# Low parts of two weight operands per pair: from a VectorE subtraction to a ScalarE negation and an adding DMA

## The chip, the cores and the metric

The kernel runs on one NeuronCore of a Trainium2 chip. The metric is the device time of one launch in microseconds, as the median of several runs. The engines are named as the profile names them: PE (TensorE, matrix products), DVE (VectorE), ACT (ScalarE), POOL (GpSimd) and SP (SyncE, which here only issues DMAs). Each engine takes its own instructions strictly in their order and waits on semaphores of the others; an instruction that waits holds up everything behind it on its engine.

## The reference

One layer of a hybrid encoder over 512 tokens of width 1024, in float32: a token-mixing part (a bidirectional Mamba-2 scan, dilated window attention, gates, a projection), a LayerNorm, and a channel part. The change lies in the channel part alone:

```python
h = layer_norm(alpha * h + mix, ln1_g, ln1_b)
f = jnp.square(jax.nn.relu(h @ w_up)) @ w_down      # w_up: 1024 x 4096, w_down: 4096 x 1024
h = layer_norm(alpha * h + f, ln2_g, ln2_b)
```

## The kernel before

**Split operands.** PE multiplies in a reduced float32 form (fp32r). To keep the accuracy, every operand `w` is split into a high part `h`, which is `w` rounded to fp32r, and a low part `l = w - h`; a product is then three PE products, high by high, high by low and low by high. The helper `wsplit` (L1298 to L1300) makes such a pair: ACT copies (casts) the source into `h`, DVE subtracts `f32(h)` from the source into `l`.

**The pairs.** The first blocks of `w_up` are multiplied plainly. The rest go in 14 pairs of 128-column blocks, `PAIRS`, numbered n = 0 to 13. A pair is computed as a 2 x 2 block product with seven multiplications in place of eight. Its two blocks are loaded raw (`pair_load`, L1281) into `pr{n}_0` and `pr{n}_1`, tiles of 128 x 1024 in a pool of three buffers. `pair_prep(n, e)` makes the weight operands out of them in four steps:

- e = 0: `pa{n}`, high and low part of the whole of `pr{n}_0`.
- e = 1: `pb{n}`, two sums. Here `pr{n}_0` and `pr{n}_1` are changed in place by four additions on DVE (L1315, L1317, L1319, L1321), of which L1315 is the first that needs `pr{n}_1`; the high parts are ACT casts (L1316, L1320), the low parts DVE subtractions (L1318, L1322).
- e = 2: `pc{n}`, high and low part of `pr{n}_1` as it is by then (128 x 1024); after it, `pair_load(n + 1, 1)` reuses the buffer of `pr{n}_1`.
- e = 3: `pd{n}`, high and low part of the second half of `pr{n}_0` (128 x 512); after it, `pair_load(n + 2, 0)` reuses that buffer.

Steps 2 and 3 are the third and fourth operand, and both call `wsplit`.

**Their use.** `up_seg(n, 0..3)` issues the PE work of a pair: 12 matmuls of 256 columns per multiplication, eight with the high part of the weights and then four with the low part. Segment 0 uses `pa`, segment 1 `pb`, segment 2 `pc`, segment 3 `pd`. The PSUM tiles are `ps_x{n}` (two banks in turn), `ps_y` and `ps_z` (one bank each). All of a pair's x products accumulate in one tile, and its intermediate sums are read out of it on the way: ACT reads it after segment 1 (L1381) and DVE after segment 2 (L1390), and PE may go on adding to it only after that. ReLU and square are ACT operations in place (L1354, L1355, L1373, L1396, L1397).

**The down products.** Between the segments of the pairs stand the products with `w_down`, also seven to a 2 x 2 block scheme, for three chunks of 1024 hidden columns (`product`, L169 to L171: 12 matmuls of 512 columns for each half of the weights, j = 0 and j = 1). Their activations are split into `ah` and `al` (L1450 on ACT, L1451 on DVE), their weights into `ch` and `cl`, once for each j (L1456 on ACT, L1457 on DVE). The weight sums between the products are made by adding DMAs: `add_halves` (L1425) lets POOL issue a DMA that adds one raw quarter of `w_down` to another in SBUF (`wq_B` tiles, 512 KB each).

**What sets the order.** The loop at the end of the page interleaves pairs and products. PE's order is the order of the program text there. The orders of ACT, DVE, POOL and SP in this stage come from a scheduler, which at build time lists the instructions by its own estimate of when each is due; on the chip each engine then follows its list, whatever the real times are. POOL issues nothing in this stage but the adding DMAs.

Of the kernel before, what the change touches and what calls it, by code (L numbers as in the profile page):

```python
# [11 lines left out]
F32R = mybir.dt.float32r  # L12
AF = mybir.ActivationFunctionType
ALU = mybir.AluOpType
# [27 lines left out]
def f32(ap):  # L42
    return ap.bitcast(F32)
# [3 lines left out]
def hybrid_layer_kernel(ctx: ExitStack, tc: tile.TileContext, t: dict, out: bass.AP):  # L47
    nc = tc.nc
    act, dve, pool, pe, dma = nc.scalar, nc.vector, nc.gpsimd, nc.tensor, nc.sync
# [1227 lines left out]
    def pair_load(n, j):  # L1277
        if n < len(PAIRS):
            ch, b = PAIRS[n]
            raw_w[n, j] = wp.tile([P, 1024], F32, name=f"pr{n}_{j}", tag="wraw", bufs=3)  # L1280
            dma.dma_start(raw_w[n, j], t["w_up"][ch * 8 + b + j])  # L1281
# [4 lines left out]
    def slot(name):  # L1286
        if name in LENT:
            both = qp.tile([P, 2, 1024], F32R, name=name, tag=f"wq{LENT[name]}", bufs=1)
            return both[:, 0, :], both[:, 1, :]
        if name in ("pb0", "pc1"):  # L1290
            return [qp.tile([P, 1024], F32R, name=f"{name}{x}", tag=f"c{x}", bufs=2) for x in "hl"]
        s_ = slot_n[0] % 3
        slot_n[0] += 1
        if s_ < 2:
            return [wp.tile([P, 1024], F32R, name=f"{name}{x}", tag=f"w{x}", bufs=2) for x in "hl"]
        return [fp.tile([P, 1024], F32R, name=f"{name}{x}", tag=f"x{x}", bufs=1) for x in "hl"]

    def wsplit(h, l, src):  # L1298
        act.copy(h, src)
        dve.tensor_sub(l, src, f32(h))  # L1300

    K0, K1 = slice(0, 512), slice(512, 1024)

    def pair_prep(n, e):

        if n >= len(PAIRS):
            return
        r0, r1 = raw_w[n, 0], raw_w.get((n, 1))
        if e == 0:
            h, l = slot(f"pa{n}")  # L1310
            wsplit(h, l, r0)
            op_w[n, "B11"], op_w[n, "B21"] = (h, l, K0), (h, l, K1)
        elif e == 1:
            h, l = slot(f"pb{n}")
            dve.tensor_add(r0[:, K0], r0[:, K0], r1[:, K0])  # L1315
            act.copy(h[:, K0], r0[:, K0])  # L1316
            dve.tensor_add(r1[:, K0], r1[:, K0], r1[:, K1])  # L1317
            dve.tensor_sub(l[:, K0], r0[:, K0], f32(h[:, K0]))  # L1318
            dve.tensor_add(r0[:, K0], r0[:, K0], r1[:, K1])  # L1319
            act.copy(h[:, K1], r0[:, K0])  # L1320
            dve.tensor_add(r0[:, K1], r0[:, K1], r0[:, K0])  # L1321
            dve.tensor_sub(l[:, K1], r0[:, K0], f32(h[:, K1]))  # L1322
            op_w[n, "T1"], op_w[n, "T2"] = (h, l, K0), (h, l, K1)
        elif e == 2:
            h, l = slot(f"pc{n}")
            wsplit(h, l, r1)
            op_w[n, "T3"], op_w[n, "B22"] = (h, l, K0), (h, l, K1)
            pair_load(n + 1, 1)
        else:
            h, l = slot(f"pd{n}")  # L1330
            wsplit(h[:, K0], l[:, K0], r0[:, K1])
            op_w[n, "T4"] = (h, l, K0)
            pair_load(n + 2, 0)

# [174 lines left out]
    with tc.issue_after(ln_end[-1].ins):  # L1509
        pair_prep(0, 0)  # L1510
    hf_ctx.close()
    qp = wq_ctx.enter_context(tc.tile_pool(name="qp", bufs=1, side="right", reuse_waits="tile"))
    with tc.issue_after(ln_end[-1].ins):
        pair_prep(0, 1)
# [3 lines left out]
    with tc.manual_schedule(engines={mybir.EngineType.PE}):  # L1518
        up_seg(0, 0)
        pair_prep(0, 2)  # L1520
        up_seg(0, 1)
        pair_prep(0, 3)
        pair_prep(1, 0)
        up_seg(0, 2)
        load_quarter(0, "B12")
        up_seg(1, 0)
        pair_prep(1, 1)
        load_quarter(0, "B22")
        up_seg(0, 3)
        pair_prep(1, 2)  # L1530
        up_seg(1, 1)
        pair_prep(1, 3)
        ops = split(0, SEQ[0])
        pair_prep(2, 0)
        up_seg(1, 2)
        up_seg(2, 0)
        pair_prep(2, 1)
        up_seg(1, 3)
        load_quarter(0, "B21")
        sums(0, SEQ[0])  # L1540
# [161 lines left out]
```

## Time and profile before

| | |
|---|---|
| median of 3 runs | 984.01 us (983.98 to 986.72) |
| the profiled execution | 984.42 us, span of its instructions 982.7 us |
| PE busy | 972.9 us (99% of the span) |
| DVE busy | 806.5 us (82%) |
| ACT busy | 607.2 us (62%) |
| POOL busy | 76.2 us (8%) |
| granted PE clock | 0.999 of full speed |

All times inside the execution count from the span's start, in microseconds. In a row of the timeline the first number is the start, the second the duration; then come engine, line, operation, the tile written, `<-`, the tiles read, shapes, and in brackets the idle time of the engine before it with what ended it. Buffer numbers are often left out by the profile (`pr` for `pr4_1`), so a row is placed by its time. A row of SPq is the issue of a DMA; the landing time is given separately. The pairs run from about 670 to 932 us.

### The profile page before, as it was taken

The page shows a single profiled execution, that of the slowest core. Times are in us where ns is not written, and L with a number is a line of the kernel's source. Part 1 is how long each engine was busy: PE and PEld are TensorE (multiplying, and loading weights), DVE is VectorE, ACT ScalarE, POOL GpSimd, SP SyncE. Part 2 cuts the span into 40 slices and gives each one's busy share as a digit, 9 for nine tenths or more (in the row PEclk, how much of TensorE's full clock was granted, in tenths as well). Part 3 has the DMA queues.
Part 4 walks back from the last instruction along what each step waited for, and adds up shares of the span by engine and source line. Part 5 has one row for each costly group of instructions (what it writes and reads, how often), then busy time and mean ns, then how long its engine had stood idle before and what let it go on. Part 6 is the DMA issues. An engine that isn't in the chain of part 4 may idle for free.

```text
span 982.7 us, 14783 instructions
## 1 busy us (share of the span) xinstructions
PE 972.9 (99%) x5447; PEld 835.1 (85%) x5447; DVE 806.5 (82%) x1235; ACT 607.2 (62%) x1149; POOL 76.2 (8%) x79
## 2 busy tenths in 40 slices
PE   9999999999999999999999999999999999999997
PEld 6988888888888888788778888899989998989986
DVE  7986998798998899997798258498898898898757
ACT  6664796469856995694775344147666666656620
POOL 0100100120011101202000000000200110110000
PEclk9999999999999999999999999999999999999999
DMA  9666476335652485474773248313953854671322
GB/s 355 152 146 171 127 199 199 97 116 153 214 151 90 149 243 147 123 234 140 252 237 111 79 149 313 127 44 125 242 148 131 213 129 171 176 169 44 110 83 86
DMA packets 57992, 155.94 MB, mean 159 GB/s; under 512 B 7488, under 2 KB 10432, under 8 KB 57664
## 3 DMA queue, kind: packets, MB, share of 16 engines
q1 hardware_dynamic: 53072, 139.04, 43.9%
q0 software_dynamic: 4560, 15.44, 8.6%
q8 instruction: 43, 0.70, 0.3%
q10 hardware_dynamic: 288, 0.52, 0.1%
q14 instruction: 29, 0.24, 0.1%
HBM read 128.25 MB, written 12.44 MB: 143 GB/s over the span
## 4 chain that ended last, share of the span: by engine, by line
PE 86%; DVE 8%; ACT 3%; DMA 2%; issue 1%; DVEq 0%; SPq 0%; ACTq 0%
PE ps_pa L159 9%; PE ps_z L159 8%; PE ps_x L159 8%; PE ps_x L1341 8%; PE ps_z L1341 4%; PE ps_k L159 3%; PE ps_g L159 3%; PE ps_q L159 3%; PE ps_pX L169 2%; PE ps_pX L170 2%; PE ps_pX L171 2%; PE ps_y L1341 2%; PE ps_vX L351 2%; PE ps_u L159 2%; PE ps_pZ L169 2%; PE ps_pZ L170 2%
## 5 line engine op out<-in xcount | busy, mean ns | idle before, releaser
L110 DVE TENSOR_TENSOR wl<-wraw,wh 128x1024 fp32r<-128x1024 f32 x103 | 129.7, 1265 | 57.4 <-ACT wh L109 42.2
L109 ACT CAST wh<-wraw 128x1024 fp32r<-128x1024 f32 x103 | 107.2, 1045 | 73.9 <-PE ps_o L171 13.2
L1457 DVE TENSOR_TENSOR cl<-wq_B,ch 128x1024 fp32r<-128x1024 f32 x42 | 51.2, 1220 | 14.8 <-ACT ch L1456 14.3
L1456 ACT CAST ch<-wq_B 128x1024 fp32r<-128x1024 f32 x42 | 44.1, 1050 | 24.0 <-PE ps_pX L171 16.6
L159 PE MATMUL ps_pa<-yh,wh 128*128 128x512 f32 x128 | 51.7, 404 | 0.0
L1425 POOL DMA_DIRECT2D wq_B<-wq_B x24 | 20.6, 856 | 391.2 <-DMA wq_B<-in_w_dn_dram 225.4
L159 PE MATMUL ps_g<-xh,wh 128*128 128x512 f32 x128 | 50.6, 396 | 0.0
L159 PE MATMUL ps_z<-xh,wh 128*128 128x512 f32 x128 | 50.4, 393 | 0.0
L159 PE MATMUL ps_g<-xl,wh 128*128 128x512 f32 x128 | 49.9, 390 | 0.0
L159 PE MATMUL ps_z<-xl,wh 128*128 128x512 f32 x128 | 49.9, 389 | 0.0
L159 PE MATMUL ps_pa<-yl,wh 128*128 128x512 f32 x128 | 48.4, 393 | 0.0
L724 ACT ACTIVATE U<-bc,acr 128x128 f32<-128x128 f32 x128 | 42.3, 391 | 8.9 <-DMA bc<-dr_acr 7.7
L159 PE MATMUL ps_x<-xh,wh 128*128 128x512 f32 x120 | 47.2, 394 | 0.0
L159 PE MATMUL ps_x<-xl,wh 128*128 128x512 f32 x120 | 46.7, 389 | 0.0
L522 DVE SCALAR_TENSOR_TENSOR acc<-ps_x,vec,acc 128x510 f32<-128x510 f32 (+1 forms) x60 | 44.5, 742 | 0.7 <-ACT acc L520 0.3
L726 DVE SCALAR_TENSOR_TENSOR U<-bc,acr,U 128x128 f32<-128x128 f32 x128 | 43.2, 375 | 0.8 <-ACT U L724 0.8
L730 ACT ACTIVATE G<-cb,tok 128x128 f32<-128x128 f32 x128 | 41.7, 391 | 0.0
L169 PE MATMUL ps_pX<-ch,ah 128*128 128x512 f32 x96 | 37.6, 392 | 0.0
L170 PE MATMUL ps_pX<-cl,ah 128*128 128x512 f32 x96 | 37.6, 392 | 0.0
L171 PE MATMUL ps_pX<-ch,al 128*128 128x512 f32 x96 | 37.3, 389 | 0.0
L1450 ACT CAST ah<-r 128x1024 fp32r<-128x1024 f32 x21 | 22.1, 1053 | 20.6 <-PE ps_pX L170 14.3
L159 PE MATMUL ps_pa<-yh,wl 128*128 128x512 f32 x128 | 34.8, 392 | 0.0
(884 smaller groups left out, 2841.2 us busy)
## 6 DMA issues: line engine op xcount, KB each, us to landing
wraw<-in_w_in_dram SPq DMA_DIRECT2D x66, 512.0 KB, 3.8
bc<-dr_acr SPq DMA_DIRECT2D x64, 256.0 KB, 4.4
pr<-in_w_up_dram SPq DMA_DIRECT2D x28, 512.0 KB, 5.5
wq_B<-in_w_dn_dram SPq DMA_DIRECT2D x24, 512.0 KB, 4.5
wq_B<-wq_B POOLq DMA_DIRECT2D x24, 512.0 KB, 4.7
be<-dr_ear SPq DMA_DIRECT2D x32, 256.0 KB, 5.1
wraw<-in_w_ps_dram SPq DMA_DIRECT2D x16, 512.0 KB, 4.2
dr_gate<-g SPq DMA_DIRECT2D x16, 256.0 KB, 2.8
```

What stands on the lines that cost most here:

```text
L109: a = act.copy(h[:, :width], r[:, :width])
L110: v = dve.tensor_sub(l[:, :width], r[:, :width], f32(h[:, :width]))
L159: ins = pe.matmul(ps, l, r, start=(first and n == 0), stop=(last and n == len(seq) - 1))
L169: pe.matmul(ps, lh, rh, start=(first and i == 0), stop=False, skip_group_check=not check)
L170: pe.matmul(ps, lh, rl, start=False, stop=False, skip_group_check=not check)
L171: ins = pe.matmul(ps, ll, rh, start=False, stop=(last and i == n - 1), skip_group_check=not check)
L522: dve.scalar_tensor_tensor(acc[:, o0:o1], ps[:, i0:i1], w(k), acc[:, o0:o1], op0=ALU.mult, op1=ALU.add)
L724: act.activation(U[:, ch(c)], bb[:, ch(c)], AF.Identity, bias=acr[:, c, 32 + h:33 + h])
L726: dve.scalar_tensor_tensor(U[:, ch(c)], bf[:, ch(c)], acr[:, c, h:h + 1], U[:, ch(c)], op0=ALU.subtract, op1=ALU.min)
L1341: pe.matmul(ps[:, LO], w_[:, wk], src[:, x, k0 + k, cs], start=(first and i == 0), stop=(i == 11), skip_group_check=not first)
L1456: act.copy(h, w[:, j, :])
L1457: dve.tensor_sub(l, w[:, j, :], f32(h))
```

## The change

In steps 2 and 3 of `pair_prep`, `wsplit` is replaced by a new helper, `dma_split`. The high part is cast by ACT as before. The low part is made in two steps: ACT writes the negated high part into `l`, and then a DMA that POOL issues adds the raw source onto it in SBUF (`l = -h + src`). The DVE subtraction is gone, 14 of 128 x 1024 and 14 of 128 x 512.

```diff
@@ -1299,6 +1299,11 @@
         act.copy(h, src)
         dve.tensor_sub(l, src, f32(h))
 
+    def dma_split(h, l, src):
+        act.copy(h, src)
+        act.activation(l, f32(h), AF.Copy, scale=-1.0)
+        pool.dma_start(l, src.bitcast(F32R), accum_op=ALU.add)
+
     K0, K1 = slice(0, 512), slice(512, 1024)
 
@@ -1323,12 +1328,12 @@
         elif e == 2:
             h, l = slot(f"pc{n}")
-            wsplit(h, l, r1)
+            dma_split(h, l, r1)
             op_w[n, "T3"], op_w[n, "B22"] = (h, l, K0), (h, l, K1)
             pair_load(n + 1, 1)
         else:
             h, l = slot(f"pd{n}")
-            wsplit(h[:, K0], l[:, K0], r0[:, K1])
+            dma_split(h[:, K0], l[:, K0], r0[:, K1])
             op_w[n, "T4"] = (h, l, K0)
             pair_load(n + 2, 0)
```

From L1301 on, the changed kernel's lines stand five higher: its L1320 is L1315 of before, its L1395 is L1390, its L1430 is L1425; the three lines of `dma_split` are L1303 to L1305. PE's order is the same. The orders of the other engines are scheduled anew, and move at three places that matter below.

ACT, around the third operand of pair 1, before (`v` is the copy of a PSUM tile, `ch` a high part of `w_down`):

```order
L1380 COPY v_0_6699<-ps_z_6674 128x256
L1299 CAST pc1h<-pr_1_6672 128x1024
L1456 CAST ch_6845<-wq_B_6633 128x1024
L1381 ACTIVATE v_0_6700<-ps_x_6639 128x256
L1320 CAST pb1h<-pr_0_6611 128x512
L1299 CAST pd_6836<-pr_0_6611 128x512
```

and of the change:

```order
L1385 COPY v_0_6700<-ps_z_6675 128x256
L1321 CAST pb1h<-pr_0_6611 128x512
L1386 ACTIVATE v_0_6701<-ps_x_6639 128x256
L1303 CAST pc1h<-pr_1_6673 128x1024
L1461 CAST ch_6849<-wq_B_6633 128x1024
L1325 CAST pb1h<-pr_0_6611 128x512
L1304 ACTIVATE pc1l<-pc1h 128x1024
```

The negation that starts the low part of `pc1` stands behind a cast for the down product and behind the second cast of `pb1`, not right behind its own cast.

DVE, around the second operand of pair 2, before:

```order
L1300 TENSOR_TENSOR pa2l<-pr_0_6707,pa2h 128x1024
L1315 TENSOR_TENSOR pr_0_6707<-pr_0_6707,pr_1_6805 128x512
L1317 TENSOR_TENSOR pr_1_6805<-pr_1_6805 128x512
L1318 TENSOR_TENSOR pb2l<-pr_0_6707,pb2h 128x512
L1319 TENSOR_TENSOR pr_0_6707<-pr_0_6707,pr_1_6805 128x512
L1321 TENSOR_TENSOR pr_0_6707<-pr_0_6707 128x512
L1300 TENSOR_TENSOR pc2l<-pr_1_6805,pc2h 128x1024
L1391 TENSOR_TENSOR r_1_6638<-ps_z_6807,v_1_6833 128x256
L1322 TENSOR_TENSOR pb2l<-pr_0_6707,pb2h 128x512
L1390 SCALAR_TENSOR_TENSOR r_1_6638<-ps_x_6744,v_1_6832 128x256
```

and of the change:

```order
L1300 TENSOR_TENSOR pa2l<-pr_0_6709,pa2h 128x1024
L1320 TENSOR_TENSOR pr_0_6709<-pr_0_6709,pr_1_6808 128x512
L1322 TENSOR_TENSOR pr_1_6808<-pr_1_6808 128x512
L1396 TENSOR_TENSOR r_1_6638<-ps_z_6810,v_1_6836 128x256
L1323 TENSOR_TENSOR pb2l<-pr_0_6709,pb2h 128x512
L1395 SCALAR_TENSOR_TENSOR r_1_6638<-ps_x_6746,v_1_6835 128x256
L1324 TENSOR_TENSOR pr_0_6709<-pr_0_6709,pr_1_6808 128x512
L1462 TENSOR_TENSOR cl_6854<-wq_B_6633,ch_6853 128x1024
L1326 TENSOR_TENSOR pr_0_6709<-pr_0_6709 128x512
L1327 TENSOR_TENSOR pb2l<-pr_0_6709,pb2h 128x512
```

The subtraction of `pc2` is gone, and the read of `ps_x` of pair 1 (L1395, before L1390) stands four rows behind the first addition that needs `pr2_1`. In pairs 4, 5, 9 and 13 that first addition (L1315) keeps its place between the two read-outs of a finished down product, in front of `al` and `cl` of the next; in pairs 8 and 12 it moves behind them.

POOL, in the same stage, of the change (before, only the rows of L1425 stand there):

```order
L1430 DMA wq_B_7252<-wq_B_7325 128x1024
L1430 DMA wq_B_7325<-wq_B_7464 128x1024
L1430 DMA wq_B_7252<-wq_B_7325 128x1024
L1430 DMA wq_B_7325<-wq_B_7464 128x1024
L1305 DMA pc6l<-pr_1_7601 128x1024
L1305 DMA pd6l<-pr_0_7436 128x512
L1430 DMA wq_B_7252<-wq_B_7464 128x1024 x2
```

The adding DMA of `pc6` stands behind four additions of the second chunk's quarters, `pc10` likewise in the third chunk. On SP the load of `pr{n+1}_1` now waits for the landing of the adding DMA of `pc{n}`, and that of `pr{n+2}_0` for the one of `pd{n}`; before, both waited for the DVE subtraction.

## The prediction

> **What bounds the kernel now.** I read the page's busy times first, then the busy times by stretch over the stage of the pairs, then the chain of waits. Columns of a stretch: its length, then busy time (and instructions) of PE, weight loads, DVE, ACT, POOL, the granted clock, the busy share of the DMA engines, GB/s.
>
> ```profile
> PE 972.9 (99%) x5447; PEld 835.1 (85%) x5447; DVE 806.5 (82%) x1235; ACT 607.2 (62%) x1149; POOL 76.2 (8%) x79
> ...
> 660.00:930.00 270.00, 270.00 (x1756) 247.71 (x1755) 233.20 (x296) 173.43 (x259) 20.55 (x24) 1.00 0.54 149
> ...
> 700.00:710.00 10.00, 10.00 (x64) 9.04 (x63) 8.89 (x9) 5.70 (x7) 1.69 (x2) 1.00 1.03 268
> 780.00:790.00 10.00, 10.00 (x58) 8.79 (x58) 10.00 (x14) 5.30 (x9) 1.73 (x3) 1.00 0.71 157
> ...
> 700.31 1.44 PE ps_x L1341 x12
> ```
>
> PE is busy for 270.00 of the 270 us that hold all the pairs, at full clock, and the chain of waits there is PE alone: 12 matmuls of 256 columns in 1.44 us, one multiplication after another. DVE is busy for 233.20 of it and in places without a gap (780 to 790), but it delivers in time. So this stage lasts as long as PE's matmuls. DVE time that is saved buys nothing unless PE waits somewhere for DVE, and the stretch shows no such wait; an operand that comes too late costs its whole lateness. The question is therefore one of lateness.
>
> **What is removed and added.** Prices from the groups by line, by shape, and from the queries by tile:
>
> ```profile
> L1300 DVE TENSOR_TENSOR pc<-pr,pc x1: 1216/1216/1216, 670.5 to 670.5; 128x1024 fp32r<-128x1024 f32 x1
> L1300 DVE TENSOR_TENSOR pd0l<-pr,pd0h x1: 693/693/693, 673.7 to 673.7; 128x512 fp32r<-128x512 f32 x1
> L109 ACT CAST wh<-wraw 128x1024 fp32r<-128x1024 f32 x103 | 107.2, 1045 | 73.9 <-PE ps_o L171 13.2
> L1354 ACT ACTIVATE r<-r 128x512 f32<-128x512 f32 x13 | 8.2, 633 | 9.7 <-DVE r L1391 9.7
> L1425 POOL DMA_DIRECT2D wq_B<-wq_B x24: 847/856/908, 690.7 to 876.1; - x24
> DMA to landing us min/median/max: 4.4/4.7/8.4
> DMA to landing us min/median/max: 3.5/5.7/6.9
> q0 software_dynamic: 3456, 12.58, 26.2%
> ```
>
> DVE loses 14 x 1.22 + 14 x 0.69 = 26.7 us. No row shows a negation of 128 x 1024; between a cast of that size (1.05) and an ACTIVATE of half of it (0.63) I take 1.05 and 0.63, so ACT gains 14 x 1.68 = 23.5 us, 9% of the stage on top of 64%. That is room enough, and PE hides it. POOL issues 28 more adding DMAs at 0.86 us. The first landing row is of the 24 additions of `w_down` quarters (512 KB each, same kind), the second of the loads of `pr`. The last row is the queue of the additions from 660 to 920 us: 24 of them take 26.2% of the DMA engines' 260 us, 2.84 us each. The new ones take 14 x 2.84 + 14 x 1.42 = 60 us of them, and the DMA share of the stage goes from 0.54 to about 0.76, with single stretches already at 1.03. So I take 5.5 us for an addition of 512 KB (bounds 4.4 and 8.4) and 5 for a load of `pr` (3.5 and 6.9; the low end is a load alone).
>
> The low part of `pc` was finished 1.22 us after its cast. Now it takes 1.05 for the negation, what the scheduler put in front of that on ACT, and 5.5: some 5.3 us more. The low part of the next operand is not the worst of it. SP may load `pr{n+1}_1` only when the addition has read `pr{n}_1`, and L1315, the first addition of the next pair's sums, waits for that load, with DVE's queue behind it.
>
> The Trainium skill, page "DMA: Bandwidth & Descriptors", section "Anatomy of one DMA — SWDGE (gpsimd) path", fits a DMA from that queue as 2.0 us plus its bytes over 436 GB/s: an estimate of 3.2 us for 512 KB. No addition here landed under 4.4, so the measured row is used; by the page's figure all the lateness below would fit into the slack.
>
> **First term: the start, pairs 0 to 2.** No product stands between the first segments, so slack is small.
>
> ```profile
> 670.30 0.60 ACT L1242 ACTIVATE r<-ps_u 128x512 f32<-128x512 f32 x1 [0.81 <-PE ps_u L159]
> 671.76 0.33 SPq L1281 DMA_DIRECT2D pr<-in_w_up_dram  x1
> 678.57 0.69 DVE L1315 TENSOR_TENSOR pr<-pr,pr 128x512 f32<-128x512 f32 x1
> 683.70 0.33 SPq L1281 DMA_DIRECT2D pr<-in_w_up_dram  x1
> wq_B<-in_w_dn_dram SPq DMA_DIRECT2D x2, 512.0 KB, 5.8
> 689.25 0.69 DVE L1315 TENSOR_TENSOR pr<-pr,pr 128x512 f32<-128x512 f32 x1
> 688.63 1.12 PE L1341 MATMUL ps_z<-S,pb1h 128*128 128x256 f32 x8
> 692.47 0.64 PE L1341 MATMUL ps_z<-S,pc1l 128*128 128x256 f32 x4
> 694.76 0.42 DVE L1390 SCALAR_TENSOR_TENSOR r<-ps_x,v 128x256 f32<-128x256 f32 x1
> 697.27 1.60 PE L1341 MATMUL ps_x<-ht,pd 128*128 128x256 f32 x12
> 700.15 1.12 PE L1341 MATMUL ps_x<-S,pb2h 128*128 128x256 f32 x8
> ```
>
> Pair 0: the negation stands behind the ReLU of 670.30, runs to 671.85, the addition lands at 676.6 (4.7, little else is in flight), and the load of `pr1_1` goes then instead of at 671.76; it lands 3.7 later, 680.3, so L1315 of pair 1 moves from 678.57 to 680.3. PE needs `pb1`, made of these sums, only from 688.63 and does not notice. Pair 1: five DVE steps of 0.65, the cast of `pb1`'s second half (0.62) and the negation end at 685.2. Two loads of quarters are in flight, which took 5.8 each; I give the addition 6.0: 691.3. PE wants `pc1`'s low part at 692.47, 1.2 to spare. The load of `pr2_1` moves from 683.70 to 691.3 and lands at 696.3, so L1315 of pair 2 is 7 us late (689.25). In the new DVE order the read of `ps_x` (L1390) is the fourth behind it: 0.69 + 0.6 + 0.34 + 0.6 + 0.42 puts its end at 698.9, and PE may add `pd1` to that tile, at 697.27, only afterwards: 1.6 us lost. Behind it come L1319, `cl` and L1321 (0.6, 1.14, 0.6) and ACT's cast of `pb2`'s second half (0.6): 702.2 instead of the 700.15 at which PE wants it, 2.05 in all, which holds the 1.6. I put **2.0 us**. With 4.4 and 3.5 it is 0 (693.2 + 5.9 is before 700.15), with 8.4 and 6.9 it is 6.3. The DMA of `pd1` starts by 686.5 and has until 698.2, behind eight high matmuls of 0.12: hidden, and so are the later `pd`, whose segment 3 comes a product later; without that cover each would cost its 5.5.
>
> **Second term: DVE held up between products, pairs 4, 5, 9, 13.** Pair 5 stands for them:
>
> ```profile
> 740.04 0.36 ACT L1371 COPY v<-ps_x 128x256 f32<-128x256 f32 x1
> 741.44 0.33 SPq L1281 DMA_DIRECT2D pr<-in_w_up_dram  x1
> 748.89 0.69 DVE L1315 TENSOR_TENSOR pr<-pr,pr 128x512 f32<-128x512 f32 x1
> 750.05 0.64 PE L1341 MATMUL ps_x<-ht,pc4l 128*128 128x256 f32 x4
> 751.30 1.22 DVE L1457 TENSOR_TENSOR cl<-wq_B,ch 128x1024 fp32r<-128x1024 f32 x1
> 752.13 0.23 PE ps_pZ L169
> ```
>
> `pc4`'s negation follows the copy that ends at 740.40 and ends at 741.45; the addition lands at 747.0 (PE wants it at 750.05: hidden), the load at 752.0, so L1315 starts 3.1 late and with it `al` and `cl` behind it. `cl` ended at 752.52; it is for the second half of the product of 752.13, which begins 12 matmuls of 0.23 later and uses it at 755.1. Slack 2.6, loss 0.5. But what the blocked DVE hands to ACT late (ReLUs, casts) also delays the next `pc`, so I take **1.2 us** at each of the four places, **4.8** together. Bounds: 0 (4.4 and 3.5 make it 0.5 late), and 5.3 each, 21 in all. Pairs 8 and 12 have L1315 moved behind `cl`: 0.
>
> **Third term: POOL's queue, pairs 6 and 10.**
>
> ```profile
> 779.55 0.86 POOL L1425 DMA_DIRECT2D wq_B<-wq_B  x1 [5.10 <-DMA wq_B<-wq_B]
> 786.61 0.64 PE L1341 MATMUL ps_x<-ht,pc6l 128*128 128x256 f32 x4
> ```
>
> The addition of `pc6` stands behind this one, which waits 5.10 us for another to land. It leaves at 780.41 at the earliest, lands at 785.9, and PE wants it at 786.61: 0.7 to spare, and up to 2.2 lost at 8.4. With the addition in front still moving I take **0.5** each, **1.0**.
>
> Sum: 2.0 + 4.8 + 1.0 = 7.8 us on the span of 982.7. The execution itself took 984.42, 1.72 more than its span and 0.41 more than the median: 990.5 + 1.72 - 0.41 = 991.8, **992 us**.
>
> **Rivals.** A measurement of this kernel tells 0.3% (3 us) from no change; the forecast is 0.8% above the median.
>
> Hidden: additions land in 4.4 and loads in 3.5 to 4, all lateness fits the slack, and PE never waits: 984 to 986. For it: the median addition took 4.7 and DVE's own queue gets lighter. Against it: the stage's DMA share rises by two fifths. It decides when the two together stay under about 8.5 us. This is also what the page's formula would give.
>
> Cascade: the loop from one pair's L1315 to the next is longer than a pair lasts on PE.
>
> ```profile
> 728.08 1.11 PE L1341 MATMUL ps_x<-ht,pc3h 128*128 128x256 f32 x8
> 749.10 1.11 PE L1341 MATMUL ps_x<-ht,pc4h 128*128 128x256 f32 x8
> 753.21 0.63 ACT L1354 ACTIVATE r<-r 128x512 f32<-128x512 f32 x1 [0.86 <-DVE r L1391]
> 758.59 1.05 ACT L1299 CAST pc5h<-pr 128x1024 fp32r<-128x1024 f32 x1
> ```
>
> A pair lasts 21.0 (728.08 to 749.10). The loop: L1315 to the ReLU 4.3, from there to the end of the cast 6.4, a small read 0.4, negation 1.05, addition 5.5, load 5: 22.7. If nothing in it gave way, all 11 pairs from 3 on would lose 1.7 each, 18.7, with the start 20.7: 1005. Against it: between those casts ACT waits for PE or DVE (0.86 at the ReLU), and this idle time is slack.
>
> Faster: a wait for DVE that the records hide. Matmuls of 256 columns go at 0.120 us (1.44 over 12), the 512 wide ones at 0.23, half of which is 0.115. If the 0.005 came from operands arriving just in time from a crowded DVE, the 14 x 84 matmuls of the pairs could win up to 6 us: 978. It would decide from 3 us on, half of the excess. Against it:
>
> ```profile
> 743.83 0.76 PE L1341 MATMUL ps_z<-S,pb4h 128*128 128x256 f32 x5
> 744.43 0.64 PE L1341 MATMUL ps_z<-S,pb4l 128*128 128x256 f32 x4
> 744.76 1.23 DVE L1457 TENSOR_TENSOR cl<-wq_B,ch 128x1024 fp32r<-128x1024 f32 x1 [2.42 <-ACT ch L1456]
> ```
>
> DVE has been idle for 2.42 us before 744.76, so it had nothing left to deliver, and the five matmuls in that time still take 0.60, 0.120 each.
>
> **Chances.** Forecast (987 to 1000) 0.58, hidden 0.21, cascade 0.17, faster 0.04. So slower by over 0.3%: 0.75, within: 0.21, faster: 0.04. The forecast's own range is 987 to 1000; to hold eight in ten the range takes in the upper part of hidden and the lower two thirds of cascade: 984.5 to 1010.
>
> **What would show it.** Right: PE idle for 5 to 12 us between 690 and 930, put down to DVE's read of `ps_x` (L1395) near 697, to `cl` or `al` near the second halves of products, to the adding DMA of `pc6` and `pc10`; DVE idle in front of L1320, released by the DMA of `pr`; 28 additions at L1305 with a median landing near 5.5. Wrong: no idle time on PE (hidden), idle time in every pair (cascade), landings under 4.4 or over 8.4, or matmuls at another pace.

## The result

| | before | changed |
|---|---|---|
| median | 984.52 us (983.98 to 986.72) | 1020.11 us (1018.64 to 1022.96) |
| ratio | | 1.0361 [1.0333, 1.0389] |
| span of the profiled execution | 982.7 us | 1018.1 us |

The change makes the kernel 36 us slower, 3.6%. That is outside the predicted range (984.5 to 1010) and far above the forecast of 992. The page's busy times and the stretches of the changed kernel, same columns as before:

```profile
PE 984.4 (97%) x5447; PEld 843.0 (83%) x5447; DVE 783.5 (77%) x1207; ACT 624.5 (61%) x1177; POOL 100.5 (10%) x107
...
660.00:930.00 270.00, 247.46 (x1533) 224.54 (x1533) 186.61 (x238) 167.70 (x252) 41.13 (x48) 0.96 0.71 175
700.00:710.00 10.00, 8.91 (x50) 8.38 (x51) 7.74 (x11) 9.19 (x17) 2.54 (x3) 0.83 0.71 162
780.00:790.00 10.00, 8.45 (x60) 7.76 (x58) 3.05 (x3) 3.80 (x5) 0.86 (x1) 1.00 1.05 279
```

PE, without a gap before, is idle for 22.5 of 270 us, and its granted clock, 1.00 before, is 0.96 on average. Both losses have a number. The waits of PE from 640 us on (what it waited for, us in total, times, the longest) add up to the idle time:

```profile
PE ps_x L1346 <- DVE r L1395: 12.3, 3, 4.9
PE ps_pZ L170 <- DVE cl L1462: 5.0, 3, 2.1
PE ps_x L1346 <- DMA pc2l<-pr: 2.1, 1, 2.1
PE ps_x L1346 <- DMA pc11l<-pr: 0.9, 1, 0.9
...
DVE pr L1320 <- DMA pr<-in_w_up_dram: 36.7, 10, 6.8
```

The last row is DVE's own: ten times its first sum (L1320, before L1315) stood in front of a load of `pr` that had not landed, 36.7 us in all. PE's order is the same in both kernels, so the same matmul can be looked up in both timelines, and the difference of its two starts grows from place to place. That gives the whole bill:

| place (time in the changed kernel) | lost, us | of it half clock |
|---|---|---|
| ahead of 655, where the kernels don't differ | 1.2 | |
| pair 1, read of `ps_x` (701) | 4.2 | 1.5 |
| pair 2, `pc2` low part (716) | 3.9 | 1.5 |
| `cl` behind the blocked sum of pair 4 (746) | 4.0 | 1.6 |
| `cl`, pair 5 (770) | 1.6 | |
| read of `ps_x` behind the blocked sum of pair 6 (793) | 7.2 | 2.0 |
| `cl`, pair 9 (859) | 1.8 | |
| the same read, pair 10 (882) | 6.9 | 2.0 |
| `pb7`, `pb11`, `pc3`, `pc11` | 4.6 | |
| sum | 35.4 | 8.6 |

Of the 34.2 us behind the first row, 22.5 are idle time and 8.6 half clock. The other 3.1 lie at the gaps themselves, some 0.2 at each: the start of the matmul behind a gap moves by a little more than the gap shows (at 701 by 2.77, where the gap is 2.61).

The dearest place shows the mechanism in one piece. Timelines of ACT, POOL, SP, DVE and PE around 790 us, from the negation of `pc5`:

```profile
774.37 1.04 ACT L1303 CAST pc5h<-pr 128x1024 fp32r<-128x1024 f32 x1
775.59 1.05 ACT L1304 ACTIVATE pc5l<-pc5h 128x1024 fp32r<-128x1024 f32 x1
776.94 0.86 POOL L1305 DMA_DIRECT2D pc5l<-pr  x1 [19.49 <-PE ps_y L1346]
777.48 2.45 SPq L1414 DMA_DIRECT2D wq_B<-in_w_dn_dram  x2
784.20 2.75 SPq L1281 DMA_DIRECT2D pr<-in_w_up_dram  x2
791.11 0.69 DVE L1320 TENSOR_TENSOR pr<-pr,pr 128x512 f32<-128x512 f32 x1 [5.82 <-DMA pr<-in_w_up_dram]
791.72 0.68 DVE L1505 SCALAR_TENSOR_TENSOR h<-h,ps_pX 128x512 f32<-128x512 f32 x1
792.32 0.69 DVE L1322 TENSOR_TENSOR pr<-pr 128x512 f32<-128x512 f32 x1
792.92 0.42 DVE L1395 SCALAR_TENSOR_TENSOR r<-ps_x,v 128x256 f32<-128x256 f32 x1
...
793.39 2.08 PE L1346 MATMUL ps_x<-ht,pd5h 128*128 128x256 f32 x8 [4.94 <-DVE r L1395]
```

The addition took 7.2 us (776.94 to 784.14, beside two loads of quarters issued 0.5 us later), the load of `pr6_1` that waited for it 6.8. DVE's first sum of pair 6 then began at 791.11, and the read of `ps_x`, which had nothing to do with that block, stood behind it. PE wanted it at 788.45 and waited 4.94 us. Here pair 5's segment 3 follows on segment 2 with no product between.

### The profile page after: what moved, and what is told of

It is laid out like the page before. It is cut to its first block, busy times and chain, and to the rows that moved or that the text cites. A ratio compares the mean times of both kernels' runs of the same rounds, so it can differ in the third digit from the quotient of the medians.

```text
span 1018.1 us, 14900 instructions
## 1 busy us (share of the span) xinstructions
PE 984.4 (97%) x5447; PEld 843.0 (83%) x5447; DVE 783.5 (77%) x1207; ACT 624.5 (61%) x1177; POOL 100.5 (10%) x107
## 4 chain that ended last, share of the span: by engine, by line
PE 75%; DMA 10%; DVE 8%; issue 5%; ACT 2%; POOL 0%; DVEq 0%; ACTq 0%; POOLq 0%; SPq 0%
PE ps_pa L159 9%; PE ps_x L159 8%; PE ps_z L159 8%; PE ps_g L159 7%; PE ps_x L1346 4%; PE ps_k L159 3%; DMA pr<-in_w_up_dram 3%; PE ps_q L159 3%; PE ps_yo L755 2%; PE ps_vX L351 2%; PE ps_u L159 2%; PE ps_z L1346 2%; PE ps_d L171 1%; PE ps_d L169 1%; PE ps_d L170 1%
## 5 line engine op out<-in xcount | busy, mean ns | idle before, releaser
L1320 DVE TENSOR_TENSOR pr<-pr,pr 128x512 f32<-128x512 f32 x14 | 9.7, 690 | 36.7 <-DMA pr<-in_w_up_dram 36.7
L170 PE MATMUL ps_pZ<-cl,ah 128*128 128x512 f32 x72 | 29.2, 405 | 5.0 <-DVE cl L1462 5.0
```

The lines of the kernel that those rows point to most:

```text
L170: pe.matmul(ps, lh, rl, start=False, stop=False, skip_group_check=not check)
```

## The experiments

Three theories were set against each other. A: the loop through the raw buffer, as in the rows above. B: contention, the additions slow all transfers. C: ScalarE's added work. "Lost in the stage" is always the lateness of the last matmul against the kernel before, less the lateness that the profile already shows at 655 us (-0.1 to 2.7 us from run to run). For the changed kernel it is 34.2.

**1. Which operand.** Only `pd` by the adding DMA:

```diff
-            dma_split(h, l, r1)
+            wsplit(h, l, r1)
```

> The fourth operand (pd) is still made by the negation and the adding DMA; the third (pc) goes back to the VectorE subtraction. Theory A, the loop through the raw buffer (the load of the next pair's second block waits for the landing of pc's addition, the first sum of the pair waits for that load, and VectorE's queue behind it holds PE up): this loop is gone, and the load that waits for pd's addition has a whole pair to spare, so 984 to 987 us and under 1.5 us of PE idle between 660 and 966. Theory B, contention (the additions slow all other transfers): a third of the bytes is left, so a third of the 36 us, about 996. Theory C, ScalarE's added work: a third of it is left, so about 996 too, with ScalarE named in front of PE's waits.

986.54 us, ratio 1.0018 [1.0006, 1.0031]. PE's gaps between 640 and 970 us add up to 0.12, and nothing is lost in the stage.

```profile
660.00:930.00 270.00, 269.92 (x1752) 247.57 (x1753) 225.66 (x283) 181.19 (x274) 32.65 (x38) 1.00 0.63 162
```

Fourteen additions with 14 negations cost nothing when no load that is needed soon waits for them; the profiled execution is 1.3 us late already at 655 us, ahead of the stage, which is about the 0.18%. The thirds that B and C had forecast are not there, so neither is the cause by itself.

**2. Only `pc`.** The other call of `dma_split` undone instead.

> The third operand (pc) by the negation and the adding DMA, the fourth (pd) by the VectorE subtraction. Theory A: the loop is whole, and only the half-size additions that shared the DMA engines with those of pc are gone. Their median landing falls from 6.6 to about 5.3 us, and with it each turn of the loop; 1003 to 1016 us, the largest PE gaps still in front of pd5 and pd9 (the read of ps_x behind the blocked first sum of pairs 6 and 10). Theories B and C: two thirds of the cost, about 1008, but spread over all pairs and not at these places.

1016.01 us, ratio 1.0308 [1.0281, 1.0335]; 29.8 lost in the stage. Most of the 34.2 is `pc`'s, as A says; the other 4.4 appear only when both kinds of additions are there, since `pd`'s alone cost nothing. My picture of the crowd was wrong: without `pd`'s additions, `pc`'s landed no sooner (median 7.2, in the changed kernel 6.6).

```profile
DMA to landing us min/median/max: 4.5/7.2/10.0
```

PE waited less for the read of `ps_x` (2.7 us, pair 6 only), and more for the additions themselves: 4.8 us for `pc10`, 3.5 for `pc6`, 2.2 for `pc8`.

**3. ScalarE alone.** The negation stays; VectorE adds.

```diff
-        pool.dma_start(l, src.bitcast(F32R), accum_op=ALU.add)
+        dve.tensor_add(l, f32(l), src)
```

> ScalarE's negations stay, but the raw block is added onto them by VectorE, not by a DMA: ScalarE works as in the changed kernel, VectorE as in the one before, no new DMA. Theories A and B: ScalarE's 23.5 us cost nothing or next to it, 984 to 987 us. Theory C: most of the 36 us are still there, 1005 or more.

985.96 us, ratio 1.0010 [0.9999, 1.0021], nothing lost in the stage, PE busy for 270.00 of 270 with ACT at 192.03 (173.43 before). C is out: the negations are free.

**4. The loop cut.** A fourth raw buffer, for the second blocks of odd pairs:

```diff
-            raw_w[n, j] = wp.tile([P, 1024], F32, name=f"pr{n}_{j}", tag="wraw", bufs=3)
+            raw_w[n, j] = (fp if j and n % 2 else wp).tile([P, 1024], F32, name=f"pr{n}_{j}", tag="prx" if j and n % 2 else "wraw", bufs=1 if j and n % 2 else 3)
```

> The changed kernel with a fourth raw buffer: the second blocks of odd pairs have one of their own, so the load of the next pair's second block waits for the addition of a pair earlier, which landed long ago. All 28 negations and additions stay. The list of VectorE differs by some exchanges of neighbours. Theory A: the first sum of a pair no longer waits for its load; what is left is the lateness of pc's low part for PE itself (3.1 us of idle time in the changed kernel, at pc2, pc3 and pc11) and its clock: 984.5 to 991 us. Theory B: the bytes are the same, so 1010 to 1020. Theory C: the same, 1010 to 1020.

1002.43 us, ratio 1.0178 [1.0154, 1.0201]; 16.7 lost in the stage, about half. No wait of L1320 for a load is left on DVE's list, and no wait of PE for the read of `ps_x` (12.3 us before). So theory A accounts for 17.5 us, and not for all of it. PE's waits now:

```profile
PE ps_pX L169 <- ACT ch L1461: 4.0, 1, 4.0
PE ps_x L1346 <- DMA pc6l<-pr: 1.8, 1, 1.8
PE ps_x L1346 <- DMA pc10l<-pr: 1.6, 1, 1.6
PE ps_x L1346 <- DMA pc11l<-pr: 1.5, 1, 1.5
PE ps_x L1346 <- DMA pc3l<-pr: 0.8, 1, 0.8
```

The first is an addition of a `w_down` quarter at the start that landed up to 12.9 us after its issue (longest before: 8.4); the others are the low parts themselves.

**5. One blocked row.** In pairs 2, 6 and 10 the read of `ps_x` ahead of the first sum (`issue_after` queues what it encloses behind the named instruction of the same engine; `last_read` holds the read, L1395):

```diff
-            dve.tensor_add(r0[:, K0], r0[:, K0], r1[:, K0])
+            with tc.issue_after(last_read[n - 1].ins) if n in (2, 6, 10) else ExitStack(): dve.tensor_add(r0[:, K0], r0[:, K0], r1[:, K0])
```

> The changed kernel, but in pairs 2, 6 and 10 VectorE's list has the read of ps_x (L1395) ahead of the first sum of the pair (L1320), which waits for its load. In the changed kernel PE stood 2.6, 4.9 and 4.8 us in front of this read, and another 1.5, 2.0 and 2.0 us went to half clock behind these gaps. If single blocked rows are the matter, each of these 17.8 us goes and nothing takes their place: about 1002. If the length of the loop (addition, load, sums, casts, addition) sets the pace, the next thing that needs the late block becomes the wait instead, the second operand's parts (pb6, pb10) or cl: 1012 to 1020, with the same start times of L1320 to within 3 us.

1011.10 us, ratio 1.0262 [1.0232, 1.0291]; 27.2 lost in the stage, 7.0 less. Neither bound: DVE's read no longer stops PE, but other rows that the late block holds up do. At pair 6 PE waits 1.1 us for ACT's own read of `ps_x` (L1376), which stands in ACT's list behind the late casts of `pb6`, 0.4 for `pb6`'s low part and 1.0 for `pc6`'s. Idle time fell by 5.1 us and half clock by some 4 (three windows in place of seven); more gaps, though shorter ones, took 2 us of that back. L1320 still waited for its load, in pair 6 until 786.97 (791.11 in the changed kernel).

**6. The start left out.** `(dma_split if n > 2 else wsplit)` in both calls, with the fourth buffer:

> The fourth raw buffer, and the negation and addition only from pair 3 on; the operands of pairs 0 to 2 by the VectorE subtraction. With the fourth buffer alone PE still lost 16.7 us in this stage: 6.8 at 722 to 729 in front of ch, whose quarter came late from an addition that took some 10 us among two loads of pr, two of quarters and two other additions, and 9.9 in front of the low parts of pc3, pc6, pc10, pc11 and pb11. If the start is a crowd on the DMA engines made by the additions of pairs 1 and 2, its 6.8 us go: 995 to 996.5. If they come from the later pairs, they stay: 1002.

992.55 us, ratio 1.0083 [1.0067, 1.0098]; 7.4 lost in the stage, 9.3 less. The start is its own cost. PE's waits left are `pc10` 1.7, `pc6` 1.0, `pc11` 0.8, `pc8` 0.5, `pb7` 0.4.

**7. The same with three buffers.**

> The changed kernel with its three raw buffers, but the operands of pairs 0 to 2 by the VectorE subtraction. In the changed kernel 8.1 us were lost up to the last product of pair 2 (from the read of ps_x near 701 to pc2 near 716, clock included), and with the fourth buffer 9.3 us went when pairs 0 to 2 were left out. If the start is a separate cost, 8 to 9 of the 34 us go: 1010 to 1012. If the loop only settles into the same rhythm later, the same places cost the same from pair 4 on, and what was lost at the start is lost there: 1015 to 1019.

1010.30 us, ratio 1.0254 [1.0231, 1.0276]; 25.9 lost in the stage, 8.3 less. So the two parts add: the start costs 8.3 or 9.3, the reuse of the buffer 17.5 or 18.5, whichever is taken away first. The loop doesn't carry lateness on from pair to pair; each place loses its own.

**8. POOL's order.** Fourth buffer, additions of `pc2`, `pc6`, `pc10` (held in `pc_add`) ahead of the second pair of quarters' additions:

```diff
-            add_halves(b11, b22)
-            add_halves(b12, b22)
+            with tc.issue_after(pc_add[4 * ch + 2].ins): add_halves(b11, b22)
+            with tc.issue_after(pc_add[4 * ch + 2].ins): add_halves(b12, b22)
```

> The fourth raw buffer, and on POOL the additions of pc2, pc6 and pc10 two places earlier, ahead of the second pair of additions of quarters. With the fourth buffer alone these left POOL 6.2, 2.9 and 2.1 us after their negations were done, and PE waited 1.8 and 1.6 us for pc6 and pc10, with clock 3.6 and 1.9 in all. If POOL's queue is the cause, these 5.5 us go: about 997, or 990 if the late start goes too. If it is the DMA engines that are crowded, the order of issue only swaps who waits: 1000 to 1004.

1001.02 us, ratio 1.0162 [1.0145, 1.0179]; 17.0 lost in the stage (16.7 without this edit). It only swaps who waits: PE no longer stops for `pc6` and `pc10`, but for `pb7` and `pb11`, 2.1 us each and 0.9 on top. Why these come late is open.

**9. Negation and addition earlier** in the scheduler's lists, three buffers:

```diff
-        act.activation(l, f32(h), AF.Copy, scale=-1.0)
-        pool.dma_start(l, src.bitcast(F32R), accum_op=ALU.add)
+        with tc.high_priority(PRIO): act.activation(l, f32(h), AF.Copy, scale=-1.0)
+        with tc.high_priority(PRIO): pool.dma_start(l, src.bitcast(F32R), accum_op=ALU.add)
```

> The changed kernel with three raw buffers, negation and addition of all pairs moved forward in the lists of ScalarE and POOL: the negation of pc follows its cast one to three rows earlier (0.4 to 2.9 us), and the additions of pc2, pc6 and pc10 leave POOL one place earlier. If the loop sets the pace, each turn is shorter by that: some 0.5 us in eleven turns, 2.5 at pairs 6 and 10, and less half clock: 1005 to 1013. If the crowd on the DMA engines sets it, an earlier start only waits longer: 1016 to 1020.

1019.14 us, ratio 1.0349 [1.0328, 1.0370]; 33.5 lost in the stage. I expected 1005 to 1013 from the loop, and that is refuted: L1320 of pair 6 begins at 790.67 (791.11 before this edit), of pair 10 at 880.39 (880.06). Where it costs most, in pairs 5 and 9, the negation already stood 0.2 us behind its cast, and there was nothing to move. In pairs 4 and 8 it came 0.2 us sooner behind its cast, and the addition then took 8.6 and 8.8 us (7.5 and 7.7). The time lies in the range named for a crowd on the DMA engines (1016 to 1020), and these two pairs fit it; `pc2` and `pc6` don't, whose additions took 4.5 and 4.4 (10.8 and 6.4).

**10. All together**: fourth buffer, pairs 0 to 2 by VectorE, negations and additions earlier.

> Fourth raw buffer, pairs 0 to 2 by VectorE, and the negations and additions moved forward as in the run before. With the first two alone 7.4 us were lost in this stage: PE waited 1.0, 0.5, 1.7 and 0.8 us for the low parts of pc6, pc8, pc10 and pc11, 0.4 for pb7, and 1.7 us went to half clock. The two lists give pc6 and pc10 about 2.9 us, pc8 and pc11 about 0.5. If lateness of these operands is all that is left, 985 to 988. If the additions cost in another way, 992.

986.11 us, ratio 1.0018 [1.0008, 1.0027]; 1.9 lost in the stage, where the clock never halves. The stretch beside that of the changed kernel above:

```profile
660.00:930.00 270.00, 269.03 (x1745) 245.81 (x1744) 214.87 (x274) 189.38 (x283) 39.53 (x46) 1.00 0.71 177
```

With 22 of the 28 additions left, the DMA engines in this stretch are as busy (0.71) and move as much (177 GB/s) as in the changed kernel, and PE loses next to nothing. So it isn't the amount of traffic by itself that costs 34 us, but who has to wait for it. It doesn't beat the kernel before: PE had no idle time there to win.

**11 and 12. Clock.** The kernel before, with needless VectorE operations in front of the read of `ps_x` (counts by pair):

```diff
+            [dve.scalar_tensor_tensor(v5, x[:, LO], 0.0, v5, op0=ALU.mult, op1=ALU.add) for _ in range({5: 1, 9: 3, 13: 9}.get(n, 0))]
```

> The kernel before, with 1, 3 and 9 needless VectorE operations (they add zero times ps_x to v5) ahead of the read of ps_x in pairs 5, 9 and 13, and no adding DMA for pc or pd. By the order of VectorE's list the read comes 0.6, 2.3 and 4.2 us after PE wants it. If idle time of PE by itself costs clock, as in the changed kernel where half clock followed gaps of 2.1 us and more and none followed 1.5 and less, the granted clock is 0.5 for some 3.5 us after the second and the third gap and 1.00 after the first: about 10.7 us in all, 994.5. If the half clock came from the DMA traffic or the load of the chip, it stays at 1.00 and the sum is 7.1, about 991.

987.84 us, one run. The gaps were 0.55 and 2.14 us (in pair 13 the order puts down products in between and PE never waited), the clock stayed at 1.00. The same length had brought half clock twice in the changed kernel, so this spoke against idle time as the cause; the last section shows why it doesn't. With `{5: 4, 9: 7}`:

> The kernel before with 4 and 7 needless VectorE operations ahead of the read of ps_x in pairs 5 and 9, no adding DMA for pc or pd. In the first such run a gap of 2.14 us on PE brought no half clock, though the same length did in the changed kernel. Laid on the grid of 3.41 us on which all changes of the granted clock in one run lie, the gaps of six runs say: the clock is halved for the next window where PE was idle for more than about half of one (53% and more always, 50% and less never). By the order of VectorE's list the gaps are 3.2 and 5.4 us here: half clock for 3.4 us after the first and for 3.4 to 6.8 after the second, however the grid lies but for one place in twenty; 8.6 us of gaps and 3 to 5 of clock, 995 to 998. If idle time alone isn't the cause: 1.00 throughout and 992.5.

998.0 us, one run; gaps of 3.08 and 5.40, 11.6 lost in the stage, 8.5 of it idle and 2.8 in two windows at half clock. Its windows of 3.41 us around the first gap (length, PE busy, ..., granted clock):

```profile
774.51:777.92 3.41, 0.66 (x6) 0.45 (x4) 3.41 (x8) 0.65 (x2) 1.18 (x2) 1.00 0.78 154
777.92:781.33 3.41, 3.08 (x14) 3.09 (x15) 1.47 (x3) 2.73 (x5) 0.03 (x1) 0.50 0.78 154
781.33:784.74 3.41, 3.41 (x31) 3.41 (x30) 3.31 (x3) 3.33 (x7) 0.83 (x1) 1.00 0.68 125
```

There is no adding DMA of `pc` in this kernel: a gap of PE by itself halves the clock.

## Why the prediction was wrong, step by step

**What bounds the kernel, and that only lateness counts: right.** ACT's new work is as priced (1.05 to 1.07 and 0.63 by L1304's rows), and free (experiment 3). `pd` is free (experiment 1), with the cover that was named.

**The price of addition and load: right in the sum by luck, wrong in spread.** I took 5.5 and 5, 10.5 together. Over the 13 turns of the changed kernel, issue of the addition to landing of the load, the median is 10.6. That is two errors that cancel: the additions of `pc` took 6.8 at the median and the loads that waited for them 3.6. And pairs 5 and 9 took 14, pair 2 took 18.7. The landings of the additions by pair (KB, us to landing):

```profile
pc2l<-pr POOLq DMA_DIRECT2D x1, 512.0 KB, 10.8
pc3l<-pr POOLq DMA_DIRECT2D x1, 512.0 KB, 7.0
pc4l<-pr POOLq DMA_DIRECT2D x1, 512.0 KB, 7.5
pc5l<-pr POOLq DMA_DIRECT2D x1, 512.0 KB, 7.2
pc6l<-pr POOLq DMA_DIRECT2D x1, 512.0 KB, 6.4
pc7l<-pr POOLq DMA_DIRECT2D x1, 512.0 KB, 4.4
pc8l<-pr POOLq DMA_DIRECT2D x1, 512.0 KB, 7.7
pc9l<-pr POOLq DMA_DIRECT2D x1, 512.0 KB, 7.7
pc10l<-pr POOLq DMA_DIRECT2D x1, 512.0 KB, 6.8
pc11l<-pr POOLq DMA_DIRECT2D x1, 512.0 KB, 5.6
pc12l<-pr POOLq DMA_DIRECT2D x1, 512.0 KB, 4.7
```

In pairs 7, 11 and 12, with neither a load nor an addition of a quarter in flight, it is 4.4 to 5.6; in pairs 3, 6 and 10 an addition of a quarter is still in flight, and it is 6.4 to 7.0; in pairs 4, 5, 8 and 9 SP issues two loads of quarters within 1.5 us of the addition, and it is 7.2 to 7.7. The queue's row of before, q0 in the prediction, gave 2.84 us of all DMA engines for one addition; its neighbour gives 1.46 for one load of that size (27.5% of 260 us over 49 loads):

```profile
q1 hardware_dynamic: 7071, 25.71, 27.5%
```

So an addition is worth two loads on the engines. A place-by-place price, 4.4 plus what else is issued there, was to be had from these rows; one value for all places was the mistake.

**First term (start, 2.0, upper bound 6.3): measured 8.1.** The chain was right: L1320 of pair 2 at 698.35 (forecast 696.3), end of the read 701.04 (698.9), PE 2.6 late (1.6). Half clock added 1.5, and the bound had no place for the second half, 3.9 us for `pc2`, whose addition ran among two loads and four other additions and took 10.8. Experiments 6 and 7 give the start 9.3 and 8.3.

**Second term (pairs 4, 5, 9, 13; 4.8): measured 7.4** (4.0, 1.6, 1.8, 0), through `cl`, as described. Without the half clock behind pair 4's gap it is 5.8.

**Third term (POOL's queue at pairs 6 and 10; 1.0): measured 0.** In the changed kernel PE reaches these operands late enough. It is not an empty term: with the fourth buffer PE waits 1.8 and 1.6 there (experiment 4).

**The step that failed: no term for the first sum of pairs 6 and 10.** I listed the pairs in which L1315 holds DVE up, and let 6 and 10 count only for POOL's queue. There, too, L1315 stands between the two read-outs of a finished down product, and three rows ahead of the read of `ps_x`, in both kernels; and the next segment follows with no product between. The rows of before at pair 6:

```profile
769.91 0.68 DVE L1315 TENSOR_TENSOR pr<-pr,pr 128x512 f32<-128x512 f32 x1
771.75 0.42 DVE L1390 SCALAR_TENSOR_TENSOR r<-ps_x,v 128x256 f32<-128x256 f32 x1
772.99 1.12 PE L1341 MATMUL ps_x<-ht,pd5h 128*128 128x256 f32 x8
```

The slack was 0.8 us (read done at 772.17, wanted at 772.99). These two places alone cost 14.1 us. With 5.5 and 5 they would have come out 1.4 late (the addition from 776.94, the load 3.5 us sooner than measured); with 7.2 and 6.8 it was 4.9.

**The other failure: no case had the clock.** Every case priced a gap at its length. Half clock added 8.6 us to 22.5 of idle time.

**The rivals.** Hidden is out. Cascade had the right size for the loop (18.7; experiments 4 and 7 measure 17.5 and 18.5) by the wrong mechanism: it had every pair from 3 on lose 1.7, whereas five places lose 1.6 to 7.2 and the rest little, and leaving the start out hardly changes them (experiment 7: PE waits 10.0 us for the read in pairs 6 and 10, and 5.7 for `cl`; in the changed kernel 9.7 and 5.0). Faster is out: the matmuls went at 0.120 where the clock was 1.00. Of the sum, 34.2, I had 7.8; the difference is 14.1 for the two places left out, 6.1 for the start, 2.6 for the second term (1.6 of it clock), 4.6 for low parts and second operands that came late singly, less 1.0.

## What to carry to other kernels

Before a computation in SBUF is handed to a DMA, list which loads reuse the source's buffer: the DMA holds it for its whole landing time, and the next load's landing comes on top. Price that time at each place by what else is issued within a few us there, not by a median, and look for the place with the least slack behind the first instruction that waits. On a PE that is never idle, a gap of 2 us or more will often cost another 1.5 us or more of half clock, as it did here.

## What the runs showed of the hardware

**The clock is set on a fixed grid.** In the changed kernel the granted clock changes at 702.25, 705.67, 715.91, 719.33, 746.63, 750.05, 791.01, 797.83, 879.75 and 886.57: all multiples of 3.41 us apart. Windows of this grid (length, PE busy, ..., granted clock):

```profile
698.85:702.26 3.41, 1.17 (x9) 1.17 (x10) 3.18 (x7) 3.08 (x5) 0.00 (x0) 1.00 0.79 157
702.26:705.67 3.41, 3.41 (x18) 3.41 (x17) 2.42 (x4) 3.41 (x9) 1.63 (x2) 0.50 0.39 85
705.67:709.08 3.41, 3.41 (x23) 3.03 (x22) 2.33 (x2) 3.41 (x7) 0.91 (x2) 1.00 1.00 252
855.86:859.27 3.41, 1.87 (x9) 1.22 (x7) 3.41 (x5) 0.62 (x1) 0.00 (x0) 1.00 0.19 77
859.27:862.68 3.41, 3.41 (x19) 2.91 (x19) 3.34 (x7) 2.82 (x5) 0.00 (x0) 1.00 0.76 246
```

A window in which PE was idle for 2.24 us is followed by one at half clock, a window with 1.54 idle is not. Over the nine profiled executions with half clock in this stage, all 24 windows at full clock that were idle for 53% or more were followed by half clock, none at 50% or less was, and of the four between, one was. A window at half clock costs 1.5 us (256 columns in 0.213 instead of 0.120). The way back is stricter: a window at half clock was followed by full clock in all 25 cases in which PE was idle for at most 17% of it, and by another at half clock in all nine with 24% or more.

The 2.14 us of experiment 11 lay across two windows. That execution goes to half clock only at 983.26, behind its last matmuls, but changes there lie on the grid too (in the changed kernel 1016.28, 92 windows behind 702.26). Counted back from 983.26, one window ends at 853.56, inside the gap from 852.44 to 854.58: PE is idle for 1.12 us of one window and 1.03 of the next, 33% and 30%, and neither halves the clock.

The Trainium skill, page "TensorE: Matmul & The Clock Gate", section "Part 1: The HAM clock gate (the "warmup" mystery)", has the window (4096 cycles at 1.2 GHz, 3413 ns, free-running), and the grid agrees with it. Its rule of an idle window of some 3.4 us, as the point from which the clock falls, doesn't: 2.14 us of idle time in one window were enough here, and in the execution of experiment 6 1.74.

**Not settled.** Why `pb7` or `pb11` is late in most variants, and why kernels that change nothing ahead of 655 us reach that point up to 2.7 us later than the kernel before in their profiled executions.
